# Four more Strassen steps, a join by accumulating transfers, and moved side work in a decoder block on one core

## The chip, the core and the metric

One Trainium2 chip, one of its cores. A core has TensorE (matmuls, into the eight PSUM banks), VectorE, ScalarE and GpSimd (elementwise work), SyncE (which issues loads here), and 16 DMA engines between HBM and the on-chip SBUF. In the profile they are PE (with PEld for its weight loads), DVE, ACT, POOL and SP. The metric is the device time of one execution in microseconds (us).

## What is computed

One layer of a decoder block on x of 256 tokens by 4096 channels, all in float32:

```python
h = rmsnorm(x, norm_w)
proj = einsum('bsd,de->bse', h, w_in)            # 4096 -> 20480
u_p, z_p, u_c, b_c, c_c, z_c, g_logit = split(proj)
y_pool = causal_multiscale_pool(u_p, pool_w, pool_scale) * silu(z_p)
y_conv = causal_gated_shortconv(u_c, b_c, c_c, conv_w, conv_b) * silu(z_c)
br = einsum('bsnc,ncd->bsnd', stack([y_pool, y_conv]), w_branch)
gates = sigmoid(g_logit.reshape(b, s, 2, d) + gate_b)
x = x + einsum('bsd,de->bse', sum(gates * br), w_out)
return rmsnorm(x, final_norm_w)
```

The gated convolution is `b_gate * (conv_b + sum of three taps over c_gate * u)`, each tap shifted by a token. The pooling takes the mean over the last 2, 4, 8 or 16 tokens, minus the token itself, and then a 512 x 512 map per group. The norm's factor for each token does not touch the matmul's inner dimension: the kernel multiplies x by the channel weights alone, and scales the products by the factor `rin` of each token afterwards.

## The kernel before

**Units.** The output columns are worked in units of 1024 columns by all 256 tokens. A unit sums over 16 steps of 256 input channels (8 for the branch matmuls). The order is cz0, cb0, cu0, cc0 (gate path, b, u and c of the convolution's first half), cz1, cb1, cu1, cc1 (second half), pz0, pu0, pz1, pu1 (pooling), eight gate units, eight branch units, four output units.

**Steps.** Every float32 number is split into a rounded high part and the low rest, and a product is three matmuls (high by high, high by low, low by high). A step of kind P multiplies the four 512 x 128 quarters of its weights as they are: 4 quarters x 2 token halves x 3 = 24 matmuls. A step of kind S is a Strassen step: seven products in place of eight, 21 matmuls. In return it needs sums of weight quarters. Its products go into all four E banks ("sums" in the profile) and the four F banks ("shared"); a unit with S steps must join the F banks to its result at the end. P steps touch the E banks alone. A unit's text, such as `SIX5 = "PPPPPSPSPSPSPSPS"`, gives the kinds in order; steps are counted from 0 here.

**Preparation.** A step's weights are loaded by SyncE into one of three raw buffers (1 MB each). For a P step ScalarE rounds the four quarters into ring cells ("ring<-raw", `highs`) and VectorE subtracts to get the lows (`lows`). For an S step ScalarE rounds three quarters, VectorE makes four sums (tile "parts") and the lows of the three, then ScalarE rounds the sums and VectorE makes their lows ("ring<-parts"). The ring has 15 cells; a P step takes 4, an S step 3 and then 4 more. Cells come free as TensorE's program passes the groups that read them.

**Order.** Every engine runs in program order (`keep_in_program_order`), and the order is written out while the program is built: after each group of three matmuls `after_group` copies closed banks, takes an item from a queue of deferred work at every sixth matmul (`tick`, `TICK = 6`), and lets `pump` lay out preparations as far as ring cells, raw buffers and a limit of four steps ahead allow. At a unit's last step the limit is smaller where a unit is "urgent": now + `u.lead`, 2 by default, so that the work right after the unit does not queue behind too many preparations.

**The end of a unit.** `evacuate` copies the E banks to the unit's destination (E or Y) on ScalarE. `corner_sums` copies the F banks to J and makes their sums on VectorE. `combine` adds J to the destination: on VectorE, or, for a unit marked `late`, with two transfers from GpSimd's queue that accumulate (`gather`); a late unit is scaled by `rin` afterwards. Then the unit's epilogue, a list of items, goes into the queue: silu for z units (`silu_y`), the convolution of transposed data for c units (`c_epi`: transposes on TensorE, taps on ScalarE and VectorE, a product). `gap(n)` stands for n empty ticks.

**The first unit.** cz0 runs 16 P steps in the order `FIRST`. Beside it x is loaded, scaled by the channel weights and split into the stationary operands (`x_direct`, `x_sums`), and the squares of x's rows are summed for the norm (`square`, `fetch_rows`): one half of the tokens on ScalarE, one on VectorE. The first 12 steps use an extra tile ("opening"); when it closes, the tile for S sums ("parts") and a side tile are opened. The side tile holds the Strassen sums of one of two P operands (`side_items`), and is filled in cb0.

Of the kernel before, what the change touches and what calls it, by code (L numbers as in the profile page):

```python
# [15 lines left out]
P = 128  # L16
# [15 lines left out]
TAIL = 3  # L32

SIX5 = "PPPPPSPSPSPSPSPS"
FIRST = (0, 1, 8, 2, 9, 3, 10, 11, 4, 12, 13, 5, 14, 6, 15, 7)
OPENED = 12
SEVEN3 = "PPPSPSPSPSPSPSPS"
NINE = "PSPSPSPSSPSPSSPS"
# [12 lines left out]
def hybrid_block(ctx: ExitStack, tc: tile.TileContext, x, xc, prm, rows_in, w_in, pool_w, w_branch, w_out, out):  # L51
# [5 lines left out]
    def act(dst, src, func=AF.Copy, **kw):  # L57
        return pin(nc.scalar.activation(dst, src, func, **kw))  # L58
# [77 lines left out]
    def scale_col(b):  # L136
        return par[:, 96 + b:97 + b]

    opening = ExitStack()
    ctx.enter_context(opening)  # L140
    op = opening.enter_context(tc.tile_pool(name="opening", bufs=1))
# [363 lines left out]

    def seq_x(text):
        if text is FIRST:
            return [("P", i) for i in FIRST]
        ns = text.count("S")
        if ns > NS + NB:  # L510
            ss = list(range(ND, 16)) + [resident[0]]
            if ns > NS + NB + 1:
                resident[0] = 2 * ND - 3 - resident[0]
                ss = [ss[-1]] + ss[:-1] + [resident[0]]
            ps = [i for i in range(ND) if i not in ss]
            return [(c, (ss if c == "S" else ps).pop(0)) for c in text]
        return sequence(text, ND, ND + NS + NB, NB)
# [20 lines left out]
            lambda: sub(side["tile"][:, 1], sa[:, 0:4], side["tile"][:, 0].bitcast(F32)),  # L538
            lambda: move(side_d[i - ND + 2], side["tile"])]

    def silu_y(late):
        def silu(t):
            act(Y[:, t], Y[:, t], AF.Silu, **(dict(scale=rin[:, t:t + 1]) if late else {}))
        return gap(18 if late else 3) + [lambda: silu(0), None, lambda: silu(1)]

    def rescale(d):
        return gap(18) + [lambda: act(d[:, 0], d[:, 0], scale=rin[:, 0:1]), None,
# [2 lines left out]
    def conv_units(c, first):  # L550
        base = 2 * HALF + c * NU

        def b_epi(u):
            def product(t):
                stt(E[:, t], E[:, t], rin[:, t:t + 1], Y[:, t], ALU.mult, ALU.mult)
            return gap(18) + [lambda: product(0), None, lambda: product(1), None, lambda: move(g_d[c], E)]

        def c_epi(u):
            def inner(j):
                if j == 3:  # L560
                    for i in range(4):
                        act(chan(E)[:, 2 * i:2 * i + 2], bankview(i))

            def outer(j):
                act(chan(J)[:, 2 * j:2 * j + 2], bankview(j))

            def taps(j):
                v, y = chan(E)[:, 2 * j:2 * j + 2], chan(Y)
                for i in range(2):
                    b = 2 * j + i  # L570
                    kb = 8 * c + b
                    act(y[:, b], v[:, i], AF.Identity, scale=tap_col(2, kb), bias=bias_col(kb))
                for s in (1, 2):
                    for i in range(2):
                        b = 2 * j + i
                        kb = 8 * c + b
                        stt(y[:, b, s:], v[:, i, 0:T - s], tap_col(2 - s, kb), y[:, b, s:], ALU.mult, ALU.add)

            items = [lambda: move(Y, g_d[c])] + gap(6) + pairs(transposes(E, inner)) + gap(5) + pairs(transposes(Y, outer))
            for j, n in enumerate((1, 7, 8, 8)):  # L580
                items += gap(n) + [lambda j=j: taps(j)]
            return items + [None, lambda: mul(chan(E), chan(J), chan(Y)), lambda: put(y_d[1, c], chan(E))]

        u = in_unit(f"cz{c}", base + 3 * HALF, lambda u: silu_y(u.late) + (gap(4) + side_items(ND - 1) + side_items(ND - 2) if first else []),
                    FIRST if first else SIX5, dst=Y)
        u.late = not first
        in_unit(f"cb{c}", base + HALF, b_epi, TEN if c else NINE_A).late = True
        u = in_unit(f"cu{c}", base, lambda u: rescale(Y), NINE, dst=Y)
        u.late = True
        in_unit(f"cc{c}", base + 2 * HALF, c_epi, NINE_A).urgent = lambda: mul(E, E, Y)  # L590

    def pool_units(c):
        u = in_unit(f"pz{c}", HALF + c * NU, lambda u: silu_y(True) + gap(4) + band_items(c), HOST if c else SIX5, dst=Y)
        u.late = True
        in_unit(f"pu{c}", c * NU, lambda u: [], NINE_P).urgent = lambda: None

# [292 lines left out]

    def square(c):  # L890
        q = E
        act(q[:, 0], q[:, 0], AF.Square, accum_out=ssq[:, 0, c:c + 1])
        stt(q[:, 1], q[:, 1], 1.0, q[:, 1], ALU.mult, ALU.mult, accum_out=ssq[:, 1, c:c + 1])

    first_order = FIRST
    xt = Y.rearrange("p a n -> p (a n)").rearrange("p (s o c) -> p s o c", s=4, c=P)
# [201 lines left out]
    for u in units:  # L1098
        if u.name == "b0_0":
            last_pair["stack"].close()  # L1100
            open_last(F32)
        if u is names["o1"]:
            assert not fills
            more.close()
            open_side()

            j, items = ND - 1, list(queue)
            queue.clear()
            sides = (gap(HUSH) + [lambda: move(sa[:, 4:].rearrange("p o c -> p (o c)"),
                                                   m_d[j // 4][:, j % 4].rearrange("p k t -> p (k t)"))] + gap(8) + [  # L1110
                lambda: sums_s(sa), None, None, lambda: act(side["tile"][:, 0], sa[:, 0:4]), None,
                lambda: sub(side["tile"][:, 1], sa[:, 0:4], side["tile"][:, 0].bitcast(F32))])
            items += gap(len(sides) - len(items))
            sides += gap(len(items) - len(sides))
            queue.extend([lambda a=a, b=b: (a and a(), b and b()) for a, b in zip(items, sides)])
        if u is names["g0_1"]:
            bands_open.close()
        if u is last_x:
            side["stack"].close()
            more = ExitStack()  # L1120
            ctx.enter_context(more)
            pool = more.enter_context(tc.tile_pool(name="more", bufs=1))
            stages.extend(pool.tile([P, 8, P], F32, name=name) for name in ("sb", "sc"))
            queue_fills()
        if u is last:
            break
        for st in u.steps:
            assert st.prepared, (u.name, st.kind)
            run_step(u, st)
            if u.text is TEN and st.kind == "S" and st.op in x_ops[:ND] and st is not u.steps[-1]:  # L1130
                side_load(2 * ND - 3 - x_ops.index(st.op))
            state["now"] += 1
            if state["now"] == OPENED:
                opening.close()
                sums = ctx.enter_context(tc.tile_pool(name="parts", bufs=1)).tile([P, 4, NH], F32, name="parts")
                open_side()
            pump()
            if u.before and st is u.steps[len(u.steps) * 3 // 4]:
                flush()
                u.before()  # L1140
        flush()
        combine(u)
        queue.extend(u.epi(u))
        pump()
# [102 lines left out]
```

## Time and profile before

| | |
|---|---|
| time, median of 3 runs | 2356.45 us (2356.26 to 2356.69) |
| profiled execution, its time | 2356.82 us |
| profiled execution, its span | 2354.7 us |
| TensorE busy | 2340.7 us, 10424 matmuls |
| VectorE busy | 2217.8 us |
| ScalarE busy | 1542.9 us |
| GpSimd busy | 139.0 us |
| mean granted TensorE clock | 0.999 |
| HBM | 232 GB/s over the span |

Units begin on TensorE at: cz0 6.0, cb0 95.1, cu0 176.0, cc0 257.0, cz1 337.9, cb1 424.5, cu1 504.7, cc1 585.6, pz0 666.6, pu0 753.2, pz1 834.1 us from the span's start, by counting matmuls in the trace. A row of a timeline gives the start and the length in us, engine, line, operation, output and inputs by the program's names, and the count of merged instructions; in square brackets stands how long the engine had waited before and for whom. Most rows carry the line of a small helper (L58 `act`, L61 `tt`, L73 `stt`, L85 `gather`, L1026 the matmul in `multiply`), so the tiles tell what they are.

### The profile page before, as it was taken

What the parts mean: (1) busy time and instruction counts of PE and PEld (TensorE: products, weight loads), DVE (VectorE), ACT (ScalarE), POOL (GpSimd) and SP (SyncE); (2) the same over time, 40 slices, a digit from 0 to 9 for tenths busy, and PEclk for the clock granted to TensorE, in tenths of its full rate; (3) what the DMA queues carried; (4) which work ended last, traced back from release to release, by engine and by line L of the source; (5) the groups of instructions that cost most, each with busy time, mean ns of one, the idle gap of its engine ahead of it and who ended that gap; (6) DMA issues with size and microseconds to landing.
All of it is one profiled execution on the core that took longest, in us unless ns stands there. A gap on an engine that the chain in (4) does not pass through costs nothing.

```text
span 2354.7 us, 28337 instructions
## 1 busy us (share of the span) xinstructions
PE 2340.7 (99%) x10424; PEld 1938.7 (82%) x10424; DVE 2217.8 (94%) x2454; ACT 1542.9 (66%) x1841; POOL 139.0 (6%) x195
## 2 busy tenths in 40 slices
PE   9999999999999999999999999999999999999998
PEld 7888888888888888888888888888888888888886
DVE  8899989999979979979999999998999899999998
ACT  6666756766656666666677767677666566566664
POOL 0000000000001000100000000001101001000000
PEclk9999999999999999999999999999999999999999
DMA  9667655776656656656787787778767678767877
GB/s 351 231 234 248 217 201 215 251 232 233 222 207 216 219 196 213 220 198 222 242 258 254 256 265 246 250 267 283 258 225 247 254 247 282 250 206 263 260 255 279
DMA packets 95387, 569.44 MB, mean 242 GB/s; under 512 B 10320, under 2 KB 10576, under 8 KB 34832
## 3 DMA queue, kind: packets, MB, share of 16 engines
q1 hardware_dynamic: 69824, 485.39, 56.7%
q0 software_dynamic: 24848, 81.01, 13.7%
q8 instruction: 81, 1.33, 0.2%
q10 hardware_dynamic: 576, 1.24, 0.1%
q14 instruction: 58, 0.48, 0.1%
HBM read 521.46 MB, written 25.17 MB: 232 GB/s over the span
## 4 chain that ended last, share of the span: by engine, by line
PE 97%; DVE 1%; DMA 0%; ACT 0%; issue 0%; DVEq 0%; SPq 0%; ACTq 0%
PE sums L1026 70%; PE shared L1026 25%; PE shared L676 1%; PE shared L462 1%; DVE ring L61 1%; DMA raw<-in_w_branch_dram 0%; DVE parts L61 0%; DMA raw<-in_w_in_dram 0%; ACT ring L58 0%; DVE arena L61 0%; PE shared L652 0%; DVE J L61 0%; ACT E L58 0%; PE shared L653 0%; PE shared L655 0%
## 5 line engine op out<-in xcount | busy, mean ns | idle before, releaser
L1026 PE MATMUL sums<-ring,arena 128*128 128x512 f32 x7011 | 1640.7, 390 | 1.9 <-ACT E L58 1.1
L1026 PEld LDWEIGHTS sums<-ring,arena 128*128 128x128 f32 x7011 | 1315.3, 188 | 275.5 <-ACT E L58 1.5
L61 DVE TENSOR_TENSOR ring<-raw,ring 128x1024 fp32r<-128x1024 f32 (+2 forms) x887 | 962.2, 1104 | 70.4 <-ACT ring L58 69.5
L58 ACT ACTIVATE ring<-raw 128x1024 fp32r<-128x1024 f32 (+3 forms) x682 | 785.5, 1192 | 210.2 <-PE sums L1026 98.5
L58 ACT ACTIVATE ring<-parts 128x512 fp32r<-128x512 f32 (+1 forms) x683 | 510.4, 761 | 510.2 <-DVE parts L61 438.3
L1026 PE MATMUL shared<-ring,arena 128*128 128x512 f32 x2241 | 541.1, 389 | 0.0
L61 DVE TENSOR_TENSOR ring<-parts,ring 128x1024 fp32r<-128x1024 f32 (+1 forms) x475 | 524.5, 1146 | 8.7 <-ACT ring L58 8.7
L1026 PEld LDWEIGHTS shared<-ring,arena 128*128 128x128 f32 x2241 | 420.6, 188 | 87.3
L61 DVE TENSOR_TENSOR parts<-parts,raw 128x512 f32<-128x512 f32 x444 | 303.3, 683 | 0.0
L61 DVE TENSOR_TENSOR parts<-raw 128x1024 f32<-128x1024 f32 x222 | 270.2, 1217 | 10.9 <-DMA raw<-in_w_in_dram 6.0
L61 DVE TENSOR_TENSOR J<-J 128x512 f32<-128x512 f32 (+1 forms) x90 | 78.1, 868 | 6.0 <-ACT J L58 2.8
L1026 PE MATMUL sums<-ring,last_pair 128*128 128x512 f32 x306 | 76.2, 389 | 0.0
L58 ACT ACTIVATE J<-shared 128x512 f32<-128x512 f32 x128 | 69.5, 601 | 1.6
L1026 PEld LDWEIGHTS sums<-ring,last_pair 128*128 128x128 f32 x306 | 57.4, 188 | 11.9
L85 POOL DMA_DIRECT2D E<-J x28 | 34.2, 1463 | 479.5 <-ACT ring L58 300.1
L1026 PE MATMUL shared<-ring,last_pair 128*128 128x512 f32 x216 | 51.9, 389 | 0.0
L1026 PE MATMUL shared<-ring,side 128*128 128x512 f32 x207 | 50.7, 389 | 0.0
L1026 PEld LDWEIGHTS shared<-ring,last_pair 128*128 128x128 f32 x216 | 40.5, 188 | 8.4
L1026 PEld LDWEIGHTS shared<-ring,side 128*128 128x128 f32 x207 | 38.9, 188 | 8.1
L58 ACT ACTIVATE E<-sums 128x512 f32<-128x512 f32 x76 | 41.8, 592 | 4.5 <-PE sums L1026 2.7
L85 POOL DMA_DIRECT2D Y<-J x12 | 14.7, 1458 | 265.1 <-ACT ring L58 138.5
L58 ACT ACTIVATE E<-sums,rin 128x512 f32<-128x512 f32 x20 | 13.0, 689 | 13.9 <-PE sums L1026 13.9
(140 smaller groups left out, 645.6 us busy)
## 6 DMA issues: line engine op xcount, KB each, us to landing
raw<-in_w_in_dram SPq DMA_DIRECT2D x318, 1024.0 KB, 4.9
raw<-in_w_branch_dram SPq DMA_DIRECT2D x64, 1024.0 KB, 5.4
raw<-in_w_out_dram SPq DMA_DIRECT2D x64, 1024.0 KB, 4.8
E<-J POOLq DMA_DIRECT2D x28, 512.0 KB, 8.6
E<-in_rows_dram POOLq DMA_DIRECT2D x14, 512.0 KB, 9.8
Y<-J POOLq DMA_DIRECT2D x12, 512.0 KB, 9.3
gates_d<-E POOLq DMA_DIRECT2D x6, 1024.0 KB, 6.1
y_d<-E POOLq DMA_DIRECT2D x8, 512.0 KB, 5.2
```

What stands on the lines that cost most here:

```text
L58: return pin(nc.scalar.activation(dst, src, func, **kw))
L61: return pin(nc.vector.tensor_tensor(out=dst, in0=a, in1=b, op=op))
L85: return pin(nc.gpsimd.dma_start(dst, src, accum_op=ALU.add))
L462: pin(nc.tensor.transpose(shared(j)[:, i * T + t * P:i * T + (t + 1) * P], src[:, t, c:c + P], ident))
L676: pin(nc.tensor.matmul(o, a, b, start=(k, i) == (0, 0), stop=(k, i) == (3, 2)))
L1026: pin(nc.tensor.matmul(ps, lhs, rhs, start=n == 0, stop=n == u.total[b] - 1))
```

## The change

- In cz0 the steps at places 12 and 14 (inputs 14 and 15) become S steps. So the unit has F banks to join; it is marked late, its join is made by accumulating transfers, and silu scales by `rin` and comes 18 ticks later instead of 3. The tile for the sums is opened at the start.
- The z units cz1 and pz0 run a new text with seven S steps instead of six.
- Both halves of the rows' squares go to ScalarE.
- In cb0 the side sums begin at tick 9, beside the wait for silu, and no longer after it.
- The c units cc0 and cc1 may prepare three steps ahead instead of two at their last step; in their epilogue the first transposes come two ticks later, the second ones stay.

```diff
+SEVEN5 = "PPPPPSPSSPSPSSPS"
+FIRST_S = (14, 15)
...
+    sums = ctx.enter_context(tc.tile_pool(name="parts", bufs=1)).tile([P, 4, NH], F32, name="parts")
...
-            return [("P", i) for i in FIRST]
+            return [("S" if i in FIRST_S else "P", i) for i in FIRST]
...
-    def silu_y(late):
+    def silu_y():
         def silu(t):
-            act(Y[:, t], Y[:, t], AF.Silu, **(dict(scale=rin[:, t:t + 1]) if late else {}))
-        return gap(18 if late else 3) + [lambda: silu(0), None, lambda: silu(1)]
+            act(Y[:, t], Y[:, t], AF.Silu, scale=rin[:, t:t + 1])
+        return gap(18) + [lambda: silu(0), None, lambda: silu(1)]
...
-            items = [lambda: move(Y, g_d[c])] + gap(6) + pairs(transposes(E, inner)) + gap(5) + pairs(transposes(Y, outer))
+            items = [lambda: move(Y, g_d[c])] + gap(8) + pairs(transposes(E, inner)) + gap(3) + pairs(transposes(Y, outer))
...
-        u = in_unit(f"cz{c}", base + 3 * HALF, lambda u: silu_y(u.late) + (gap(4) + side_items(ND - 1) + side_items(ND - 2) if first else []),
-                    FIRST if first else SIX5, dst=Y)
-        u.late = not first
+        def z_epi(u):
+            items = silu_y()
+            if first:
+                sides = gap(8) + side_items(ND - 1) + side_items(ND - 2)
+                items = [lambda a=a, b=b: (a and a(), b and b()) for a, b in zip(items + gap(len(sides) - len(items)), sides)]
+            return items
+
+        u = in_unit(f"cz{c}", base + 3 * HALF, z_epi, FIRST if first else SEVEN5, dst=Y)
+        u.late = True
...
-        in_unit(f"cc{c}", base + 2 * HALF, c_epi, NINE_A).urgent = lambda: mul(E, E, Y)
+        u = in_unit(f"cc{c}", base + 2 * HALF, c_epi, NINE_A)
+        u.urgent, u.lead = (lambda: mul(E, E, Y)), 3
...
-        u = in_unit(f"pz{c}", HALF + c * NU, lambda u: silu_y(True) + gap(4) + band_items(c), HOST if c else SIX5, dst=Y)
+        u = in_unit(f"pz{c}", HALF + c * NU, lambda u: silu_y() + gap(4) + band_items(c), HOST if c else SEVEN5, dst=Y)
...
-        act(q[:, 0], q[:, 0], AF.Square, accum_out=ssq[:, 0, c:c + 1])
-        stt(q[:, 1], q[:, 1], 1.0, q[:, 1], ALU.mult, ALU.mult, accum_out=ssq[:, 1, c:c + 1])
+        for t in range(2):
+            act(q[:, t], q[:, t], AF.Square, accum_out=ssq[:, t, c:c + 1])
...
-                sums = ctx.enter_context(tc.tile_pool(name="parts", bufs=1)).tile([P, 4, NH], F32, name="parts")
```

## The prediction

> **What bounds the kernel now.** I read the page's busy shares first, then what TensorE waited for, then the stretches that the change touches, and last VectorE in order of time there.
>
> ```profile
> span 2354.7 us, 28337 instructions
> PE 2340.7 (99%) x10424; PEld 1938.7 (82%) x10424; DVE 2217.8 (94%) x2454; ACT 1542.9 (66%) x1841; POOL 139.0 (6%) x195
> PE 97%; DVE 1%; DMA 0%; ACT 0%; issue 0%; DVEq 0%; SPq 0%; ACTq 0%
> ```
>
> The chain of waits that ended last is 97% TensorE. A busy TensorE row could still hide stalls, because ends of matmuls are modelled, so the pace and the waits have to be seen.
>
> ```profile
> PE shared L873 <- DVE warm L869: 1.1, 1, 1.1
> PE sums L1026 <- ACT E L58: 1.1, 1, 1.1
> PE sums L1026 <- DVE ring L774: 0.8, 1, 0.8
> ```
>
> TensorE's whole list of waits: three, 3.0 us together, two of them before its first real matmul. The pace, from TensorE's timeline in the first unit (start, duration, count):
>
> ```profile
> 67.92 16.48 PE L1026 MATMUL sums<-ring,arena 128*128 128x512 f32 x72
> 84.24 1.07 PE L1026 MATMUL sums<-ring,last_pair 128*128 128x512 f32 x4
> ```
>
> 72 matmuls from 67.92 to 84.24 are 0.2267 us each. A P step (24 matmuls) is then 5.44 us, an S step (21) 4.76 us. TensorE is saturated: nothing becomes faster unless a matmul goes away, and new work on another engine costs time only where TensorE starves. The next engine, by stretches (TensorE, its loads, VectorE, ScalarE, GpSimd):
>
> ```profile
> 365.00:426.00 61.00, 61.00 (x271) 50.51 (x270) 60.06 (x73) 40.56 (x53) 1.51 (x2) 1.00 0.59 215
> 748.00:829.00 81.00, 81.00 (x359) 67.09 (x358) 79.41 (x92) 55.34 (x65) 11.90 (x30) 1.00 0.65 215
> ```
>
> These are the last two thirds of unit cz1, and unit pu0, which follows pz0. VectorE is busy 98% in both. So the place to look is VectorE there.
>
> **Removed matmuls.** Four P steps become S steps: two in cz0, one each in cz1 and pz0. Each drops 3 matmuls: 12 x 0.2267 = 2.72 us of TensorE, all on the path. This is certain; what has to be found is how much of it is given back.
>
> **What an S step costs VectorE.** cz1's second half on VectorE's timeline:
>
> ```profile
> 365.26 2.36 DVE L61 TENSOR_TENSOR ring<-raw,ring 128x1024 fp32r<-128x1024 f32 x2 [1.52 <-ACT ring L58]
> ...
> 369.12 1.22 DVE L61 TENSOR_TENSOR parts<-raw 128x1024 f32<-128x1024 f32 x1
> ...
> 373.19 2.35 DVE L61 TENSOR_TENSOR ring<-parts,ring 128x1024 fp32r<-128x1024 f32 x2
> 375.47 2.35 DVE L61 TENSOR_TENSOR ring<-raw,ring 128x1024 fp32r<-128x1024 f32 x2
> 377.74 1.67 DVE L73 SCALAR_TENSOR_TENSOR Y<-E,par,Y 128x255 f32<-128x255 f32 x4
> 379.32 1.22 DVE L61 TENSOR_TENSOR parts<-raw 128x1024 f32<-128x1024 f32 x1
> ...
> 406.60 2.28 DVE L61 TENSOR_TENSOR E<-J,Y 128x2048 f32<-128x2048 f32 x1
> 408.80 2.35 DVE L61 TENSOR_TENSOR ring<-raw,ring 128x1024 fp32r<-128x1024 f32 x2
> ...
> 417.42 2.42 DVE L61 TENSOR_TENSOR ring<-raw,ring 128x512 fp32r<-128x512 f32 x3
> ```
>
> An S preparation runs from 369.12 to 375.47: 6.35 us (sums and first lows until 373.19, then the lows of the sums, 2.28). A P preparation runs from 375.47 to 377.74: 2.27 us. A set of convolution taps is 1.58 (377.74 to 379.32), the final product 2.20. So an exchanged step adds 6.35 - 2.27 = 4.08 us to VectorE, and takes 0.68 us from TensorE's cover.
>
> **cz1.** VectorE has work almost without a break from step 6 (365.26) to the end, so delays add up. I lay the new order end to end from 375.47, where the two texts still agree. Steps 8 to 15 are S P S P S S P S; behind 375.47 the four-tap groups 1 to 3 and the product fall where the queue's ticks put them. Five S, three P, three taps, one product: 31.75 + 6.81 + 4.74 + 2.20 = 45.50, so step 15 is prepared at 420.97. Before it was at 417.42 (its row above: the next preparation starts). TensorE:
>
> ```profile
> 414.28 5.60 PE L1026 MATMUL sums<-ring,last_pair 128*128 128x512 f32 x24
> 419.72 2.20 PE L1026 MATMUL sums<-ring,arena 128*128 128x512 f32 x9
> ```
>
> Step 15 started at 419.72, 2.3 us after its preparation; now it would start 0.68 earlier, at 419.04. A closing S takes its last prepared cell third: that cell's low part is read by its eighth matmul, 7 x 0.2267 = 1.59 us in, at 420.63. VectorE is then not done until 420.97, or 421.3 if the wait of 0.30 for ScalarE in front of the last pair (pz0's row below) comes up here too. I take 0.5 us of stall; ends 0 (the lead at 375.47 is better by a little) and 1.5 (VectorE waits for ScalarE in front of several S steps). The step before it (P, ready 414.62, start 413.60) reads its second half 2.7 us after its start, and is in time.
>
> **cb1, behind it.** It starts some 3 us poorer (the same count as for pu0 below). Its text is P S S over and over: VectorE 2.27 + 2 x 6.35 = 14.97, TensorE 5.44 + 2 x 4.76 = 14.96. It neither gains nor loses, so it can only starve where it is already at its edge; I take 0 (up to 1).
>
> **pz0 and pu0.** pz0 is cz1 again (the same texts, taps and product); I take 0.5 (0 to 1.5). pu0 inherits the smaller lead, while VectorE also builds the pool bands:
>
> ```profile
> 752.90 2.36 DVE L61 TENSOR_TENSOR ring<-parts,ring 128x1024 fp32r<-128x1024 f32 x2 [0.30 <-ACT ring L58]
> ...
> 782.51 2.36 DVE L61 TENSOR_TENSOR ring<-raw,ring 128x1024 fp32r<-128x1024 f32 x2 [0.47 <-ACT ring L58]
> ...
> 812.91 2.35 DVE L61 TENSOR_TENSOR ring<-parts,ring 128x1024 fp32r<-128x1024 f32 x2
> ```
> ```profile
> 813.68 1.52 PE L1026 MATMUL sums<-ring,last_pair 128*128 128x512 f32 x6
> ```
>
> Its step 12 (S) was ready at 815.26, 1.58 us after TensorE began it at 813.68. That is allowed: the first pair of sum cells is read as low from the eleventh matmul (2.27 in), and VectorE finishes that pair 1.14 before the rest, so the limit is 2.27 + 1.14 = 3.41 us late. VectorE arrives in pu0 later by 420.97 - 417.42 = 3.55, loses the waits of 0.30 and 0.47 that it has today, and TensorE is 0.68 - 0.5 = 0.18 earlier: 2.96 less lead. Step 12 is then 1.58 + 2.96 = 4.54 late: 1.1 us of stall (0 to 2.5).
>
> **cz0.** Its step 12 has a lead of 7 us: TensorE begins it 24 matmuls after 67.92, at 73.36.
>
> ```profile
> 62.98 1.22 DVE L73 SCALAR_TENSOR_TENSOR E<-E 128x1024 f32<-128x1024 f32 x1
> 64.12 2.29 DVE L61 TENSOR_TENSOR ring<-raw,ring 128x2048 fp32r<-128x2048 f32 x1
> 72.10 1.05 ACT L58 ACTIVATE E<-E 128x1024 f32<-128x1024 f32 x1
> 96.99 1.22 DVE L61 TENSOR_TENSOR ring<-raw,ring 128x1024 fp32r<-128x1024 f32 x1 [5.22 <-ACT ring L58]
> ```
> ```profile
> 426.72 2.68 DVE L61 TENSOR_TENSOR J<-J 128x512 f32<-128x512 f32 x3
> ```
>
> Step 12's preparation ends at 66.4. The S form adds 4.08, but three squares (1.14 each, 62.98 to 64.12) leave VectorE before it: the lead stays above 6. Step 14 must wait for ring cells that step 12 frees at 75.4, then ScalarE's rounding and the lows: near 80, still 3 us ahead. SyncE's load for step 15 waits until step 12's preparation is laid out, which is now the freeing of a ring cell later, at 62.5 (the end of step 9) and 25 us before TensorE needs it. The squares cost ScalarE, busy 66%, 4 x 1.05 more; what covers them is those leads, and without them each would cost its 1.05. The join adds four copies on ScalarE and three sums on VectorE (2.68, as at the start of cb1, 426.72) into VectorE's gap of 5.22 before 96.99. ScalarE must still copy the first bank before cb0's first matmul; I reckon 0.5 to 1 us to spare, and take 0 (up to 2).
>
> **Transfers and side sums.** Two accumulating transfers go through GpSimd's queue at the end of cz0.
>
> ```profile
> Y<-J POOLq DMA_DIRECT2D x12, 512.0 KB, 9.3
> ```
>
> They land in about 9.3 us; silu now comes 19 ticks of six matmuls (25.8 us) in, and the next transfer in that queue, the side chunk, nine ticks (12 us). Silu leaves ScalarE's busy first steps of cb0. The side sums keep their count and end two ticks earlier. All this runs beside TensorE: 0; a landing that took over 25 us would hold up ScalarE, which rounds every step, and cost up to 2. The tile for the sums only moves in memory: no instruction, 0.
>
> **c units, one step more.** No row of TensorE's waits lies at the ends of cc0 and cc1, so there is nothing to win. A preparation of 2.2 us slips ahead of the join and of the product that the transposes read; the transposes move back two ticks, 2.72 us, which covers it. 0, at most 1.
>
> **The sum.** -2.72 + 0.5 + 0.5 + 1.1 = -0.6 on the span: 2354.1. The profiled execution took 2356.82, with 2.1 around its span, 0.37 above the median of 2356.45. By the median: 2355.8. Ends: -2.7 and, with about half of the upper ends, +4.
>
> **Rivals.** *All of it comes through.* The leads of 2 to 3 us absorb the extra VectorE work because scattered waits vanish: 2356.45 - 2.72 = 2353.7. For it: today's list of waits is empty there. Against it: 98% busy.
>
> *VectorE becomes the bound from cz1 to pu0 (slower).* If nothing absorbs an exchanged step, its unit grows by 4.08. Twice that, less cz0's 1.36, is +6.8: 2363.3. It decides the sign at 0.2% (4.7 us, about what a measurement can tell from no change) when stalls sum to over 7.4 us, so when these units absorb less than 2.1 of the 9.5 us that VectorE falls behind. Against it: cz1 alone showed 2.3 + 1.6 us of room at its end.
>
> *A stall long enough to drop the clock.*
>
> ```profile
> 5.98 16.55 PE L1026 MATMUL sums<-ring,arena 128*128 128x512 f32 x63 [0.83 <-DVE ring L774]
> 1718.30 1.90 PE L1026 MATMUL sums<-ring,arena 128*128 128x512 f32 x7 [1.07 <-ACT E L58]
> ```
> ```profile
> 1400.00:1800.00 400.00, 398.93 (x1768) 330.16 (x1767) 385.21 (x422) 274.16 (x325) 30.13 (x42) 1.00 0.76 256
> ```
>
> The gap of 1.07 us left the granted clock at 1.00, and my stalls are no longer. The first 63 matmuls, after an idle start, took 16.55 us against 63 x 0.2267 = 14.3: about 2.2 us for one cold start. If cz0's join stalled TensorE by 3 us and cost such a start, the time would be 2355.8 + 3 + 2.2 = 2361.0. [...]
>
> **How the numbers follow.** Mine 45% (own range 2354.3 to 2357.5); all of it through 28%; stalls at the upper ends without the bound changing (2357.5 to 2361) 15%; VectorE-bound, slower 8%; the clock 2%; 2% for a gain that no row shows, since 2.72 plus the one late wait of 1.07 is still under 4.7. The range holds all but the slower cases: 2353.0 to 2360.0. Faster 0.02, same 0.90, slower 0.08.
>
> **What would show it.** TensorE with 12 matmuls fewer; new waits on VectorE's ring cells at the last step of cz1 and pz0 and at step 12 of pu0, each 1 us or less; VectorE without gaps from cz1's step 6 into cu1. I am wrong if TensorE waits at the end of cz0, or if the waits sum to more than 5 us.

## The result and the profile after

| | before | after |
|---|---|---|
| time, median of 20 runs | 2356.82 us (2356.09 to 2358.80) | 2361.20 us (2359.25 to 2363.66) |
| ratio, 95% interval | | 1.0018 (1.0012 to 1.0025) |
| profiled execution, its time | 2356.82 us | 2359.28 us |
| profiled execution, its span | 2354.7 us | 2357.6 us |
| TensorE busy, matmuls | 2340.7 us, 10424 | 2338.8 us, 10412 |

The changed kernel is slower by 4.4 us, 0.18%, just under the 0.2% of the prediction, but surely slower, since the interval excludes 1. The forecast of 2355.8 was 5.4 us too low, and the measured time lies 1.2 us above the upper end of the range. One number has to be kept apart from the start: the profiled execution took only 2.46 us more than the one before, and the medians differ by 4.4. There are two effects.

From the page of the changed kernel: span, busy shares, and the shares of the chain of waits that ended last.

```profile
span 2357.6 us, 28375 instructions
...
PE 2338.8 (99%) x10412; PEld 1935.8 (82%) x10412; DVE 2231.0 (95%) x2479; ACT 1553.7 (66%) x1866; POOL 141.8 (6%) x197
...
PE 88%; DVE 6%; issue 1%; ACT 1%; DMA 0%; DVEq 0%; ACTq 0%
```

The 12 matmuls are gone, TensorE is still 99% busy, and yet the chain is on TensorE for 88% instead of 97%. A busy share does not show the loss, the chain hints at it. Next, what TensorE waited for in the changed kernel (us in total, times, longest):

```profile
PE sums L1036 <- ACT Y L60: 2.4, 1, 2.4
PE sums L1036 <- DVE ring L784: 1.4, 1, 1.4
PE sums L1036 <- DVE ring L63: 1.3, 2, 1.1
PE sums L1036 <- ACT E L60: 1.2, 2, 0.7
PE shared L883 <- DVE warm L879: 1.1, 1, 1.1
```

The row on `DVE ring L63` (two waits) holds the small stalls that were forecast. Those on L784, on tile E and on L879 were there before, with 0.8, 1.1 and 1.1 us. The first row is new and was not forecast: 2.4 us, for ScalarE, at tile Y, which is the destination of cz0. In order of time, all three engines around the end of cz0 in the changed kernel (start, length, instruction; idle time before it and its releaser in brackets):

```profile
88.64 5.60 PE L1036 MATMUL sums<-ring,arena 128*128 128x512 f32 x24
...
91.15 1.22 DVE L63 TENSOR_TENSOR parts<-raw 128x1024 f32<-128x1024 f32 x1
...
92.46 1.84 ACT L60 ACTIVATE ring<-parts 128x1024 fp32r<-128x1024 f32 x2
...
94.69 0.69 DVE L63 TENSOR_TENSOR parts<-parts,raw 128x512 f32<-128x512 f32 x1
...
95.49 0.63 ACT L60 ACTIVATE ring<-parts 128x512 fp32r<-128x512 f32 x1 [1.19 <-DVE parts L63]
96.03 2.04 ACT L60 ACTIVATE Y<-sums 128x512 f32<-128x512 f32 x4
96.66 5.51 PE L1036 MATMUL sums<-ring,arena 128*128 128x512 f32 x23 [2.41 <-ACT Y L60]
```

Read it from below. TensorE starts cb0 at 96.66, when the first of four E banks has been copied to Y. ScalarE starts these copies at 96.03. Between 88.64 and the end of cz0 lie 24 matmuls, 5.44 us, so TensorE was through at 94.08 and the first banks closed before that. ScalarE was not busy: it waited 1.19 us in front of 95.49. That instruction rounds the last sum for step 1 of cb0 (an S step), a sum that VectorE ended at 95.38. The copies stand behind this rounding in program order. So TensorE waits for ScalarE, ScalarE for VectorE, and VectorE works on something that TensorE needs 5.6 us later (step 1 of cb0 begins at 102.24). The same place before the change, on ScalarE:

```profile
93.28 2.73 ACT L58 ACTIVATE Y<-sums,rin 128x512 f32<-128x512 f32 x4 [2.77 <-PE sums L1026]
```

There ScalarE had idled 2.77 us, waiting for the banks to close: every rounding was out of the way.

Why it was not now is told by the lead of VectorE, the time from the end of a step's preparation on VectorE to TensorE's first matmul of it (counted step by step in both traces, us):

| | cz0 11 | 12 | 13 | 14 | 15 | cb0 0 | cb0 1 |
|---|---|---|---|---|---|---|---|
| before | 7.8 | 7.0 | 9.4 | 9.7 | 10.5 | 10.5 | 8.8 |
| after | 8.0 | 4.2 | 5.9 | 2.0 | 2.1 | 5.4 | 2.0 |

The first S step takes 2.8 to 3.5 us of it, the second 4.2 us more. (The last two columns of "after" already contain TensorE's wait of 2.57; without it they would be smaller by that.) At 2 us of lead, the work on cb0's steps lies beside the end of cz0 and no longer ahead of it.

Up to the last matmul the changed kernel falls 2.46 us behind, as much as the profiled times differ. (The spans differ by 2.90; the other 0.44 lie behind the last matmul.) By the starts of units these 2.46 us divide so: +0.33 by step 3 of cz0 (start-up), +1.21 over the rest of cz0 (-1.36 for six matmuls, +2.57 for this wait, by counting matmuls from 88.64 to 96.66: 8.02 - 5.44), +0.13 in cb0, -0.68 in cz1, -0.13 in pz0, +1.60 in pu0, and 0.0 over all that follows.

### The profile page after: what moved, and what is told of

It is laid out like the page before. It is cut to its first block, busy times and chain, and to the rows that moved or that the text cites. A ratio compares the mean times of both kernels' runs of the same rounds, so it can differ in the third digit from the quotient of the medians.

```text
span 2357.6 us, 28375 instructions
## 1 busy us (share of the span) xinstructions
PE 2338.8 (99%) x10412; PEld 1935.8 (82%) x10412; DVE 2231.0 (95%) x2479; ACT 1553.7 (66%) x1866; POOL 141.8 (6%) x197
## 3 DMA queue, kind: packets, MB, share of 16 engines
q8 instruction: 81, 1.33, 0.2%
q10 hardware_dynamic: 576, 1.24, 0.1%
## 4 chain that ended last, share of the span: by engine, by line
PE 88%; DVE 6%; issue 1%; ACT 1%; DMA 0%; DVEq 0%; ACTq 0%
PE sums L1036 62%; PE shared L1036 24%; DVE ring L63 4%; DVE parts L63 1%; PE shared L686 1%; PE shared L465 1%; ACT ring L60 0%; DVE arena L63 0%; DVE Y L75 0%; DVE J L63 0%; DMA raw<-in_w_branch_dram 0%; DVE E L63 0%; PE shared L662 0%; ACT E L60 0%; PE shared L663 0%
## 5 line engine op out<-in xcount | busy, mean ns | idle before, releaser
L63 DVE TENSOR_TENSOR ring<-raw,ring 128x1024 fp32r<-128x1024 f32 (+3 forms) x897 | 961.3, 1091 | 70.9 <-ACT ring L60 70.3
L60 ACT ACTIVATE ring<-parts 128x512 fp32r<-128x512 f32 (+1 forms) x694 | 521.8, 762 | 553.5 <-DVE parts L63 479.0
L1036 PE MATMUL shared<-ring,arena 128*128 128x512 f32 x2277 | 549.8, 389 | 0.0
L63 DVE TENSOR_TENSOR ring<-parts,ring 128x1024 fp32r<-128x1024 f32 (+1 forms) x483 | 533.9, 1147 | 6.2 <-ACT ring L60 6.2
L1036 PEld LDWEIGHTS shared<-ring,arena 128*128 128x128 f32 x2277 | 427.4, 188 | 88.8
L63 DVE TENSOR_TENSOR parts<-parts,raw 128x512 f32<-128x512 f32 x452 | 308.8, 683 | 0.0
L63 DVE TENSOR_TENSOR parts<-raw 128x1024 f32<-128x1024 f32 x226 | 275.2, 1218 | 4.8 <-DMA raw<-in_w_out_dram 4.8
L63 DVE TENSOR_TENSOR J<-J 128x512 f32<-128x512 f32 (+1 forms) x93 | 80.7, 867 | 2.9
L60 ACT ACTIVATE E<-E 128x1024 f32<-128x1024 f32 x20 | 20.9, 1047 | 4.1 <-DMA E<-in_x_dram 4.1
```

What stands on the lines that cost most here:

```text
L63: return pin(nc.vector.tensor_tensor(out=dst, in0=a, in1=b, op=op))
L1036: pin(nc.tensor.matmul(ps, lhs, rhs, start=n == 0, stop=n == u.total[b] - 1))
```

## The experiments

The theory, **Q**: the order of ScalarE's queue at the end of cz0 is the loss; it needs S steps in cz0 (they use up VectorE's lead) and a cb0 step prepared ahead of the copies. The rival, **V**: it is the load of the engines at the end of cz0, the moved squares on ScalarE included, and not the order, that decides. A third, **R**: the waits differ between executions of the same kernel, so that a trace shows only a part of what the median holds. The expectations use these or say the same in words. All times in the table are medians of 11 runs, of 5 for the two `early_s` kernels; each is set against the runs of the kernel before that lay between its own on the same chip (2356.76, 2356.97 and 2357.03 us in the three groups).

| run | median us | minus before | ratio (95%) | TensorE's wait ahead of cb0, us |
|---|---|---|---|---|
| after_again | 2361.30 | +4.5 | 1.0017 (1.0008 to 1.0026) | 2.6 |
| no_first_s | 2358.18 | +1.4 | 1.0004 (0.9995 to 1.0013) | none |
| sq_dve | 2362.63 | +5.9 | 1.0024 (1.0016 to 1.0033) | 2.0 |
| hold_s1 | 2357.85 | +1.1 | 1.0004 (0.9995 to 1.0013) | none |
| before_again | 2357.09 | +0.1 | 1.0004 (0.9995 to 1.0013) | none |
| six | 2360.85 | +3.9 | 1.0016 (1.0007 to 1.0024) | 4.0 |
| early_s | 2367.21 | +10.2 | 1.0045 (1.0032 to 1.0057) | 8.0 |
| early_s_pz6 | 2368.20 | +11.2 | 1.0048 (1.0036 to 1.0061) | 8.1 |
| one_s | 2359.72 | +2.7 | 1.0012 (1.0004 to 1.0021) | 0.2 |
| one_s_pz6 | 2356.97 | -0.1 | 0.9999 (0.9990 to 1.0008) | 0.2 |
| hold_pz6 | 2358.29 | +1.3 | 1.0004 (0.9995 to 1.0013) | none |
| cz1_only | 2357.93 | +0.9 | 1.0005 (0.9996 to 1.0014) | none |

An interval is about 2 us wide to each side, so differences of 1 us between single runs settle nothing; the last column does not depend on that.

**The changed kernel once more.** Edit: none (a blank).

> The changed kernel once more. The first profile of it has a span 2.9 us above before's, while its median lies 4.4 us above before's median. Theory R (thin leads let chance in): the waits of TensorE differ from the first profile's by 1 us or more in sum, and single times spread over 3 us or more. Rival (nothing varies but the chip): the same waits to 0.3 us (2.4 at the end of cz0, 0.7 at the end of pz0, 1.3 at step 12 of pu0), and 2.5 to 4.5 us above before.

Measured: the same time, and another trace. By its marks R holds: TensorE's waits sum to 9.1 us against 7.4 in the first trace (a wait of 1.70 at start-up is new), and single times spread over 3.2 us. The wait ahead of cb0 is there again, and this time something follows it. TensorE's timeline, and then stretches of the same trace (start and end, length, busy time and count of TensorE, its weight loads, VectorE, ScalarE and GpSimd, granted clock, DMA share, GB/s):

```profile
88.83 5.60 PE L1036 MATMUL sums<-ring,arena 128*128 128x512 f32 x24
97.07 8.70 PE L1036 MATMUL sums<-ring,arena 128*128 128x512 f32 x30 [2.63 <-ACT Y L60]
```
```profile
94.09:97.50 3.41, 0.78 (x4) 0.39 (x3) 3.34 (x6) 2.21 (x5) 0.00 (x0) 1.00 0.69 245
97.50:100.91 3.41, 3.41 (x10) 2.64 (x9) 3.41 (x4) 2.87 (x5) 1.95 (x3) 0.50 0.73 288
```

30 matmuls take 8.70 us instead of 6.8. TensorE counts as busy from 97.07 on, but the granted clock is 0.5 for 3.41 us (the records of the clock give 97.50 to 100.91), matmuls in it are 427 ns apart instead of 227, and 1.73 us are lost. In the first profile of the changed kernel no such stretch follows the wait of 2.41. That is the second effect: after the wait of 2.63 a window of half clock came on top, after that of 2.41 none; what the traces show of when it comes stands in the last section. The 20 times of the changed kernel fit it: three lie at 2359.25 to 2359.45, none up to 2360.8, the other 17 from there on. That these 17 executions are the ones with a window was not seen in each of them, as there are two traces; it is the likely reading of 4.4 against 2.46. Their mean granted clock points the same way: 0.9975 over the 17, 0.9983 over the three, and one such window takes 1.71 / 2360 = 0.0007 out of the mean.

**No S steps in cz0.**

```diff
-FIRST_S = (14, 15)
+FIRST_S = ()
```

> The changed kernel with P steps alone in the first unit (so no join of it either); all else stays, the late silu and the squares too. Theory Q: at the end of cz0 ScalarE's copies of the E banks stand behind the rounding of the sums of cb0's step 1, which waits for VectorE; the two S steps bring 1.4 us and this costs 2.6. Then the wait of 2.4 us before cb0 is gone and the time is 1.2 us below the changed kernel's. Rival V (the squares on ScalarE are what makes ScalarE late): a wait of 1 us or more stays before cb0, and the time is above the changed kernel's by up to 1.4 us.

No wait ahead of cb0, and 3.1 us less than the changed kernel, though six matmuls (1.36 us) come back. The S steps of cz0 cost more than they save. The expectation had 1.2, the wait less the matmuls (2.57 - 1.36); that the half-clock windows went with the wait would make up the difference.

**Squares' second half back on VectorE.**

```diff
-        for t in range(2):
-            act(q[:, t], q[:, t], AF.Square, accum_out=ssq[:, t, c:c + 1])
+        act(q[:, 0], q[:, 0], AF.Square, accum_out=ssq[:, 0, c:c + 1])
+        stt(q[:, 1], q[:, 1], 1.0, q[:, 1], ALU.mult, ALU.mult, accum_out=ssq[:, 1, c:c + 1])
```

> The changed kernel with the second half of the rows' squares back on VectorE. Theory V: without 1.24 us of squares in front of the last preparations, ScalarE reaches the E banks in time: the wait before cb0 falls from 2.4 to under 1 us and the time by 1.5 us or more. Theory Q: VectorE gets the 1.14 us that ScalarE loses, the chain through both stays as long, the wait stays at 1.5 to 3.5 us.

The wait is 2.0 instead of 2.4 to 2.6, and the time no better. (Its trace holds two windows of half clock, from 20.88 and from 99.39 us on, so its time says little of the squares; the wait does.) The moved squares are not the cause, and they help as little. In the changed kernel's trace the second pair stands right in front of the rounding for step 15 (ScalarE's timeline):

```profile
81.06 1.05 ACT L60 ACTIVATE E<-E 128x1024 f32<-128x1024 f32 x1
82.01 0.19 ACT L60 ACTIVATION_READ_ACCUMULATOR E<-E 128x1 f32 x1
82.10 1.05 ACT L60 ACTIVATE E<-E 128x1024 f32<-128x1024 f32 x1
83.05 0.19 ACT L60 ACTIVATION_READ_ACCUMULATOR E<-E 128x1 f32 x1
83.15 1.99 ACT L60 ACTIVATE ring<-raw 128x1024 fp32r<-128x1024 f32 x2
```

Squares that leave VectorE make VectorE wait for ScalarE (1.53 us ahead of 84.22, where it makes the lows of these cells), because ScalarE has to round before VectorE can subtract.

**The same work in another order.** In the last two steps of cz0 no preparation beyond step 0 of cb0 is laid out, so that the copies stand ahead of cb0's step 1 in ScalarE's queue:

```diff
         if u.urgent and st is u.steps[-1]:
             state["limit"] = state["now"] + u.lead
+        if u is units[0] and st in u.steps[-2:]:
+            state["limit"] = len(u.steps)
```

> The changed kernel, but in the last two steps of cz0 nothing beyond cb0's step 0 may be laid out, so ScalarE's four copies of the E banks stand ahead of the rounding for cb0's step 1; no work is taken away. Theory Q: the wait of 2.4 us before cb0 is gone, cb0's step 1 is prepared later and may wait up to 1 us; the time is 1.4 to 2.6 us below the changed kernel's. Theory V and the theory that the join's own copies cost it: the wait stays at 1.5 us or more, as squares, copies and sums are all still there.

ScalarE's timeline of this run:

```profile
92.20 2.64 ACT L60 ACTIVATE Y<-sums 128x512 f32<-128x512 f32 x4 [0.81 <-PE sums L1036]
94.74 1.57 ACT L60 ACTIVATE ring<-raw 128x512 fp32r<-128x512 f32 x2
96.21 1.05 ACT L60 ACTIVATE ring<-parts 128x1024 fp32r<-128x1024 f32 x1
```

The copies begin at 92.20 as the first banks close, the roundings come after them, and TensorE runs through (start, length):

```profile
88.60 12.40 PE L1036 MATMUL sums<-ring,arena 128*128 128x512 f32 x54
...
140.88 1.43 PE L1036 MATMUL sums<-ring,arena 128*128 128x512 f32 x5 [0.89 <-DVE ring L63]
```

Same work on every engine, another order, 3.4 us less: Q holds and V falls. The gain is larger than the 1.4 to 2.6 expected, again by about what a half-clock window costs. cb0 begins at 94.04, 1.08 earlier than in the kernel before. But the run is not below the kernel before: VectorE's lead is still small, and at step 9 of cb0 TensorE waits 0.89 (second row), beside the deferred silu and the side sums. Holding back seems only to move the place where the lead is missing; the wait is there in the second run with this order too, and in none without it.

**The kernel before once more.** Edit: a blank in the kernel before.

> The kernel before once more, for a profile on the same chip. All four runs of this study so far lost 1.3 to 2.1 us at 17 us, in front of the third step, which the two first profiles did not. If that comes from the chip or from chance, this one shows it too; if it comes from the change (squares on ScalarE, the place of the sums' tile), it has no wait there and a time 1.3 us or more below.

Two medians of the same kernel differ by 0.1 us, while its single runs lie between 2356.1 and 2361.0. Its trace has no wait at 17 us, as the rival (the change) said, but its time is not below either. The traces of all runs speak against the change as the cause: the wait is missing in the first trace of the changed kernel and there in its second. It is there in the eight traces in which the granted clock was full early (3.8 to 5.7 us into the span), and in none of the six in which it was full late (9.6 to 10.4 us; last section).

**Six S steps in cz1 and pz0, cz0 as changed.**

```diff
-SEVEN5 = "PPPPPSPSSPSPSSPS"
+SEVEN5 = SIX5
```

> The changed kernel with the old text of six S steps in cz1 and pz0. The prediction's count: +1.36 us of matmuls, less the waits at the end of pz0 (0.4) and at pu0's step 12 (1.2 to 1.4): 0.3 to 0.5 us below the changed kernel, both waits gone, the wait before cb0 still 2 us or more. Rival (the z units' extra S steps are what costs the time): 2 us or more below.

The waits of pz0 and pu0 are gone, and the time hardly moves: the seventh steps win their 1.36 us and give it back. In this run's trace the wait ahead of cb0 is 4.01 us, and a window of half clock follows (stretches as above).

```profile
93.00:98.00 5.00, 1.03 (x5) 0.53 (x3) 4.97 (x8) 3.51 (x7) 0.00 (x0) 1.00 0.66 223
98.00:103.00 5.00, 4.96 (x15) 3.95 (x16) 4.97 (x6) 3.34 (x5) 3.08 (x3) 0.66 0.76 249
```

Up to there the program is that of the changed kernel, whose waits are 2.41 and 2.63 us. VectorE was 1.4 us later here in the middle of cz0 (it starts the same instruction at 56.27 instead of 54.90), and with so little lead a delay is passed on to TensorE.

**The S steps of cz0 earlier**, at places 11 and 13 instead of 12 and 14, to give VectorE time to catch up before the unit's end.

```diff
-FIRST = (0, 1, 8, 2, 9, 3, 10, 11, 4, 12, 13, 5, 14, 6, 15, 7)
+FIRST = (0, 1, 8, 2, 9, 3, 10, 11, 4, 12, 13, 14, 5, 15, 6, 7)
```

> The changed kernel with the two S steps of cz0 at places 11 and 13, so that two P steps end the unit and the rounding for cb0's step 1 is laid out and done well before the E banks close. Theory Q: no wait before cb0, and the time is that of the run with the held step or up to 1 us less (2356.8 to 2357.9). If ScalarE were simply overworked in cz0 (squares, join, sums), a wait of 1 us or more stays before cb0.

This expectation, that the wait would go, was wrong, and by much: 8.0 us. The lead at step 11 is only 0.3 us and at step 13 -3.5. All three engines at the end of cz0 in this run:

```profile
95.83 2.67 DVE L63 TENSOR_TENSOR J<-J 128x512 f32<-128x512 f32 x3
98.42 1.22 DVE L63 TENSOR_TENSOR parts<-raw 128x1024 f32<-128x1024 f32 x1
...
102.74 0.63 ACT L60 ACTIVATE ring<-parts 128x512 fp32r<-128x512 f32 x1 [1.15 <-DVE parts L63]
103.27 2.04 ACT L60 ACTIVATE Y<-sums 128x512 f32<-128x512 f32 x4
...
103.90 2.50 PE L1036 MATMUL sums<-ring,arena 128*128 128x512 f32 x5 [8.00 <-ACT Y L60]
```

The chain is Q's once more, with the copies right behind the rounding at 102.74, and with the three sums of the join now ahead of cb0's sums on VectorE. The miss says that the lead has to be worked out for the new place as well.

**The same with six S steps in pz0.** Edit: the one above, and

```diff
-HOST if c else SEVEN5, dst=Y)
+HOST if c else SIX5, dst=Y)
```

> As the run before, with six S steps again in pz0, whose seventh saved 0.68 and cost 0.4 + 1.3 us of waits. By the count: 1.0 to 1.2 us below it, at 2355.6 to 2356.9, so level with the kernel before or up to 1 us faster. If pu0's wait has another cause than VectorE's lead at its start, it stays and the time is 0.7 above.

The wait in pu0 is gone, the one ahead of cb0 is 8.1, and the time is within the error of the run before it, 11 us above what was expected, since that run had come out over 9 us too high. It adds nothing on the cause.

**One S step in cz0.**

```diff
-FIRST_S = (14, 15)
+FIRST_S = (14,)
```

> The changed kernel with one S step in cz0 (place 12, input 14) instead of two; the join by transfers stays. Theory Q with lead (each S step takes 4.1 us of VectorE's lead; the evacuation waits once the rounding of cb0's step 1 is later than the E banks): no wait before cb0, or under 1 us; the time is 3 to 4 us below the changed kernel's (2357 to 2358.5) although it has three matmuls more. If the join itself, and not the lead, costs the wait (copies, sums, transfers are all there): a wait of 2 us or more stays.

With one exchange the lead at steps 13 to 15 is 5.6 to 6.0 us, and the wait ahead of cb0 is all but gone (ScalarE and TensorE):

```profile
94.19 0.63 ACT L60 ACTIVATE ring<-parts 128x512 fp32r<-128x512 f32 x1 [1.10 <-DVE parts L63]
94.73 2.04 ACT L60 ACTIVATE Y<-sums 128x512 f32<-128x512 f32 x4
...
95.36 3.01 PE L1036 MATMUL sums<-ring,arena 128*128 128x512 f32 x12 [0.16 <-ACT Y L60]
```

The copies are still directly behind the rounding; it only ends 1.3 us earlier. That is Q with its size: as far as this wait goes, one S step is what the place bears. It also answers the other theory: the join's copies, sums and transfers are all there, and the wait is not. The time came out 1.2 us above the upper end of what was expected. By counting matmuls the trace has other waits: 0.5 at the end of cz1, 0.8 in pu0, 1.8 at the border of the first two branch units, 1.2 in the first output unit. The last two change from run to run (below).

**One S step in cz0, six in pz0.** Edit: the two lines together.

> One S step in cz0, seven in cz1, six in pz0: six matmuls fewer than before and, by the theory, no new wait. 1.4 us of matmuls saved: 2355.4 to 2356.4, 0.5 to 1.4 us below the kernel before. If every S step in these units costs as much as it saves, it lies at or above the kernel before.

Equal to the kernel before, with six matmuls (1.36 us) fewer, and about 0.6 us above what was expected. By its value that is the rival's case (every S step costs what it saves), but the interval holds both. Its trace again has a window of half clock, now at start-up (stretches as above):

```profile
17.00:21.00 4.00, 2.17 (x10) 1.40 (x9) 3.82 (x5) 3.62 (x7) 0.00 (x0) 1.00 1.06 414
21.00:25.00 4.00, 4.00 (x12) 3.17 (x11) 3.90 (x8) 3.01 (x4) 0.00 (x0) 0.57 0.97 369
```

**The held order, six in pz0.** Edit: those two.

> The held step before the E banks' copies, and six S steps again in pz0. Against the run with the held step alone the waits at the end of pz0 (0.4) and at pu0's step 12 (1.3) go and three matmuls come back: 1.0 us less, 2356.4 to 2357.4. If these waits are not due to pz0's seventh S step, 0.7 us more.

The waits in pz0 and pu0 are gone, the time is not lower than with the held order alone; 2.1 us of wait stand at the border of the branch units. Expectation missed.

**Only cz1's seventh step**, with the rest of the change that holds no S step (silu, side sums, c units).

```diff
-FIRST_S = (14, 15)
+FIRST_S = ()
...
-HOST if c else SEVEN5, dst=Y)
+HOST if c else SIX5, dst=Y)
```

together with the squares as before.

> From the kernel before: the seventh S step in cz1, the c units' third step ahead with the moved transposes, the late silu and the earlier side sums in cb0; no S step in cz0, six in pz0, squares as before. By the count three matmuls fewer and no wait: 0.7 us below before, inside its interval. If the moved silu or the third step ahead cost time of their own, it is 0.5 us or more above before.

By its value, +0.9 us, the expectation (0.7 below) was missed and the rival's case (0.5 or more above) met; but the interval reaches from 0.9 below to 3.3 above and holds both. So it is not shown whether the later silu, the earlier side sums or the c units' third step cost something, beyond that it is under some 3 us, and the 0.68 us of cz1's step cannot be resolved.

**What stays open.** Two waits come and go over all these runs: at the border of the branch units b0_0 and b1_0 (0.9 to 1.2 us with the kernel before, up to 2.3 with the others) and in step 15 of the first output unit (none or about 1.2). A changed count of S steps shifts the ring's cells for everything behind it, since each exchange takes three cells more of 15; whether that is the reason was not tried. No version here beats the kernel before by more than the measurement tells.

## Why the prediction was wrong

**Removed matmuls: right.** 10412, and 12 x 0.2267 = 2.72 us off TensorE. (Its busy time fell by 1.9 only; the ends of matmuls in it are modelled.)

**cz1: right in its mechanism, 0.5 us too pessimistic.** The end of cz1, TensorE and then VectorE in the changed kernel:

```profile
415.28 5.60 PE L1036 MATMUL sums<-ring,last_pair 128*128 128x512 f32 x24
420.72 2.20 PE L1036 MATMUL sums<-ring,arena 128*128 128x512 f32 x9
```
```profile
419.63 2.34 DVE L63 TENSOR_TENSOR ring<-parts,ring 128x1024 fp32r<-128x1024 f32 x2
421.90 2.34 DVE L63 TENSOR_TENSOR ring<-raw,ring 128x1024 fp32r<-128x1024 f32 x2
```

VectorE is done with step 15 at 421.97 or a little before, 1.25 us after TensorE's start on it. The limit worked out was 1.59, so there is no stall; I had put VectorE 0.7 us later against TensorE. All 0.68 us of the exchange come through in this trace; in the two runs with one S step in cz0 the same unit is 0.55 us longer, the stall that was forecast.

**cb1: right**, no wait: the unit takes 80.26 us, and took 80.24 before.

**pz0 and pu0: right in place and nearly in size, in pu0 in part by luck.** TensorE at the end of pz0 and at step 12 of pu0, then VectorE in pu0:

```profile
748.74 1.75 PE L1036 MATMUL sums<-ring,arena 128*128 128x512 f32 x7
750.74 0.73 PE L1036 MATMUL sums<-ring,arena 128*128 128x512 f32 x2 [0.24 <-DVE ring L63]
...
814.82 0.39 PE L1036 MATMUL sums<-ring,last_pair 128*128 128x512 f32 x1
816.26 1.43 PE L1036 MATMUL sums<-ring,last_pair 128*128 128x512 f32 x5 [1.06 <-DVE ring L63]
```
```profile
815.00 1.21 DVE L63 TENSOR_TENSOR ring<-raw,ring 128x1024 fp32r<-128x1024 f32 x1
```

By counting matmuls pz0 lost 0.5 us (forecast 0.5), after the seventh matmul of step 15, as worked out. Step 12 of pu0 lost 1.33 (forecast 1.1; VectorE was 4.3 late, forecast 4.54), but not at its eleventh matmul: TensorE stops after the first one, until VectorE has the lows of the raw quarters at 816.21. The second matmul already reads one of them. The forecast had set the limit by the sums' cells (3.41 late); by this cell it is 3.1, and a limit too wide and a lateness too large nearly cancelled. The unit pu0 is 1.60 longer in all. The waits gave back more than the exchanges in cz1 and pz0 won, which is why six instead of seven steps there cost nothing.

**cz0's join: the step that failed.** "I reckon 0.5 to 1 us to spare, and take 0 (up to 2)" measured 2.57 us. Unlike the ends of cz1 and pz0, the end of cz0 was not laid out row by row. Two sizes under it were wrong. The three squares that leave VectorE were counted as lead ("the lead stays above 6"); the lead at step 12 came out at 4.2. In place of the first square VectorE waited for ScalarE, which had got it and rounds ahead of every low (VectorE, changed kernel):

```profile
35.67 2.29 DVE L63 TENSOR_TENSOR ring<-raw,ring 128x2048 fp32r<-128x2048 f32 x1 [2.03 <-ACT ring L60]
```

At 54.90, with two squares gone, VectorE starts an instruction that it had started at 54.79 before. So only the third square counts: 7.0 - 4.08 + 1.14 is about 4. With the squares' second half on VectorE the lead is 4.1, the same. And step 14's "still 3 us ahead" was 2.0. Above all, the question was put to the wrong engine: I asked whether ScalarE had time for four copies more, and its idle time says yes (it idled 1.19 us in the middle of it). What counted was what stands ahead of the copies in its queue, and whom that waits for. The held order, with the same work, shows it.

Term by term, up to the last matmul of the profiled execution: cz0 +1.21 where -1.36 had been taken, cz1 -0.68 (-0.18), pz0 -0.13 (-0.18), pu0 +1.60 (+1.1), start-up +0.33 and cb0 +0.13 (nothing). That is 3.1 of the 5.4 us by which the forecast was too low, and cz0's wait is 2.57 of them. Another 0.37 is the median of before, 2356.82 over 20 runs and not 2356.45 over three. The last 1.9 lie between the profiled execution and the median.

**The clock: the second miss, in the rival with 2%.** "If cz0's join stalled TensorE by 3 us and cost such a start, the time would be 2355.8 + 3 + 2.2 = 2361.0." Measured: 2361.2. The place and the mechanism were named, and the chance was too small: it rested on one gap of 1.07 that left the clock alone and on stalls of no more than that. That the two times agree to 0.2 us is luck, since the wait was 2.57 and not 3, a window costs 1.73 and not 2.2, and pu0 lost more than forecast. Waits of 2.00 us (`sq_dve`) and 2.63 (`after_again`) ahead of cb0 and of 1.83 at start-up (`one_s_pz6`) were followed by half clock, the one of 2.41 in the first trace of the changed kernel was not.

**Transfers, side sums, c units: right, 0.** The accumulating transfers landed in 8.0 us (median of all 14; no row gives cz0's two alone), and silu began 27.7 us after cz0's were started (98.54 to 126.28).

**The rivals.** VectorE as the bound from cz1 to pu0 did not come: those units lost 2.2 us (0.55 in pz0, 1.60 in pu0) of the 9.5 by which VectorE falls behind. "All of it comes through" is out as well. The executions of 2359.25 to 2359.45 lie among the "stalls at the upper ends" (15%), though cz0's 2.57 is above its upper end of 2. The sign to watch, "I am wrong if TensorE waits at the end of cz0", was the right one.

## What to carry to other kernels

Before extra work is put into the last steps of a stage, list each in-order queue across the border in order of time, and ask of the copies that free the accumulators what stands ahead of them and for whom that waits; spare time on the copying engine proves nothing. Keep the preparation of the next stage behind these copies, or enough lead that it is done before them. Price a stall of the matmul engine as long as those here (1.83 us at start-up, 2.00 to 8.1 ahead of cb0) as itself plus a chance of a half-clock window; the one in `after_again` cost 1.73 us.

## What the runs showed of the hardware

- A stretch of half clock between full ones lasted 3.41 us, or three times that (10.24 us, after the waits of 8.0 and 8.1 us in the two runs with the S steps earlier; the mean granted clock of their profiled executions is 0.996, that of the changed kernel 0.998); the one of 3.41 in `after_again` cost TensorE 1.73 us. It came after waits of 2.00, 2.63, 4.01, 8.00 and 8.1 us ahead of cb0, and not after 2.41; at start-up it came after waits of 1.8 us in two runs (`sq_dve`, `one_s_pz6`) and not after waits of 1.8 in three others (`no_first_s`, `one_s`, `hold_pz6`). So the length of the wait alone does not decide.
- Where the wait falls may count as well. In the traces of before and of the first profile of the changed kernel the granted clock is full from 10.25 and 10.35 us into the span on (matmuls are 427 ns apart up to there and 227 after it) and stays so for 2338.130 us; in `sq_dve` the two windows of half clock begin 78.51 us apart (20.88 and 99.39). With the 3.413 and 10.240 of the half clock these are 685, 23, 1 and 3 times 3.4133 us. Cut into stretches of that length from 10.35 on, the first trace of the changed kernel has the wait of 2.41 in two:

```profile
92.27:95.68 3.41, 1.98 (x9) 1.31 (x7) 3.41 (x7) 1.92 (x4) 0.00 (x0) 1.00 0.76 296
95.68:99.10 3.42, 2.44 (x11) 2.02 (x12) 3.35 (x5) 3.42 (x7) 0.56 (x1) 1.00 0.80 249
```

  TensorE is busy for 0.58 and 0.71 of them, and the clock stays full. The wait of 2.63 in the second trace lies in one stretch, 94.09 to 97.50 (shown above), busy for 0.23 of it, and the next one runs at half clock. In `sq_dve` TensorE starts again at 97.89 after its wait of 2.00, so it is busy for 1.50 us, 0.44, of the 3.41 ahead of the half clock from 99.39. But in `six` the clock stayed full after a wait of 1.9 us near 1720 us. What decides is not shown by these traces.
- A wait at start-up need not cost anything. The granted clock became full 9.6 to 10.4 us into the span in six traces, those of before (10.25) and of the first profile of the changed kernel (10.35) among them, and after 3.8 to 5.7 us in the other eight. Where it came early TensorE only reached its wait at 17 us (1.2 to 1.8 us long) earlier, and step 3 of cz0 began at 24.4 to 25.0 us in all runs without a half-clock window there, and at 26.4 and 26.7 in the two with one.
- A square with accumulation on ScalarE holds it for 1.05 us here, from its start to that of the next instruction behind it (81.06, 82.10, 83.15 in the rows above). The rows of 1.05 for 1024 elements and of 0.19 for reading the accumulator out overlap, so their sum of 1.24 is too much.
